# Norm factors applied by ScalarE to transposed rows, residuals through identity products, and five more whole weight units in each mix layer

## The chip, the cores and the metric

The kernel runs on one core of one Trainium2 chip. Time is device time in microseconds (us) from start to end of one execution; lower is better. The engines are TensorE (PE, with its weight loads PEld), VectorE (DVE), ScalarE (ACT), GpSimd (POOL) and SyncE (SP), which here issues most DMA transfers.

## What is computed

A batch of 256 tokens of width 1024 in fp32 goes through a hybrid state-space and attention block, and then through two layers. What this case touches is the second part, cut to its core:

```python
def layer_norm(x, g, b):
    xc = x - jnp.mean(x, axis=-1, keepdims=True)
    var = jnp.mean(xc * xc, axis=-1, keepdims=True)
    return xc * lax.rsqrt(var + LN_EPS) * g + b

h = layer_norm(x, ln_in_g, ln_in_b)
for i in range(2):
    proj = h @ w_in[i] + b_in[i]                       # a, g (512 each), q, k, v
    conv_out = conformer_conv(a, g, ...)               # gate, 31 taps, norm, silu
    attn_out = neighbourhood_attention(q, k, v, rpb[i])
    mix = jnp.concatenate([conv_out, attn_out], -1) @ w_out[i] + b_out[i]
    h = layer_norm(ALPHA * h + mix, ln1_g[i], ln1_b[i])
    f = swiglu(h, ...) if i == 0 else moe_swiglu(h, ...)   # 8 experts, top 2
    e = jax.nn.sigmoid(h @ ple_gate_w[i] + ple_gate_b[i]) * (p[i] @ ple_w[i])
    h = layer_norm(ALPHA * h + f + e, ln2_g[i], ln2_b[i])
```

## The kernel before

Tokens lie in two blocks of 128 rows (`tb`), and every norm works on one block at a time. Weights come from HBM in units of 1 MB (128 x 2048 numbers), in the order in which they are used. `prepare` (L286 to L301) has SP issue the load of a unit into one of three raw buffers; a buffer is free for a later unit when its last reader is done. Most units are *split*: ACT casts each half to a rounded part `whi` (L298), DVE subtracts to get the rest `wlo` (L299), and each product is three fast products (`mm3`, L317 to L319: `hi x whi`, `hi x wlo`, `lo x whi`). After a split the raw buffer is free again. Units listed in `WHOLE` stay as they are: the product is one plain fp32 product that reads the raw buffer (L329 in `f_out`, L351 in `t_jobs`). `f_out` makes 128 output columns for all 256 tokens with 8 such steps; `t_jobs` makes rows of 512 columns.

A mix layer takes 19 units, numbered here from 0 (in the second layer the same numbers plus 52): 0 the per-token embedding's matrix (`ple_prod`, result `pw`); 1 to 4 the gate's two halves `a` and `g`; 5 to 8 q, k, q, k; 9 and 10 v; 11 and 12 the attention half of `w_out`; 13 and 14 its convolution half; then 15 to 18, the embedding's gate (`ple`), 15 and 16 for its first 512 columns, 17 and 18 for the others. Whole before: 1 to 4, 15 and 16.

A norm (`layer_norm`, L854 on) runs on DVE: two BN_STATS, one aggregate, a reciprocal root from some ten operations on one column (`rstd`), and two operations for each 512 columns, `(x - mean) * gain` (L869) and `* r + offset` (L870). Then `to_f` has PE transpose the block (L876, tiles `tp`), ACT copies `tp` to `hh` (L878) and casts it to `hhi`, and DVE subtracts to get `hlo`; the next layer's products read those. This happens at four places: the first norm (`b1_merge`), the norm after each mix (`ln1`), and the norm after the dense layer (`ln2`).

In `mix` the taps of the convolution (`cv`, L1012, 120 per layer on DVE) run beside the attention on PE. The convolution's own norm (L865, tile `q`) then gives the convolution half of `cat`, and `w_out`'s products accumulate in four PSUM tiles (`acc`, `acc`, `acc`, `sm`); DVE adds them to the residual `r` (L1048). The MoE begins with the gate products (`hh`, units 15 and 16, then 17 and 18 split), the router, the choice of experts on DVE (`lg`, `sel`, `pos`, ..., `posp`, `gatep`), the gather of the chosen rows by one-hot products (L1416, `oh`), and the experts' products (L1568, `raw,xn`).

A scheduler puts the written code into an order for each engine, and each engine takes its instructions in that order; the code under `high_priority` goes ahead where it can. So what stands where on an engine is read from the order listing below, not from the code.

Of the kernel before, what the change touches and what calls it, by code (L numbers as in the profile page):

```python
# [157 lines left out]
def _host(i):  # L158
# [19 lines left out]
    for l in range(2):  # L178
        a["ws2"] += _stream_mix(g["w_in_2"][l], g["w_out_2"][l], g["ple_w_2"][l], g["ple_gate_w_2"][l])
        if l == 0:  # L180
            a["ws2"] += _stream_ffn(g["ffn_w1_2"][0], g["ffn_w3_2"][0], g["ffn_w2_2"][0])
        a["cols2"].append(np.concatenate(
            [_per_part(g["b_in_2"][l])] + [_per_part(g["conv_w_2"][l][t]) for t in range(31)]
            + [_per_part(g[n][l]) for n in ("conv_b_2", "conv_ln_g_2", "conv_ln_b_2")], 1))
# [37 lines left out]
WHOLE = [a + i for a in (0, 52) for i in (1, 2, 3, 4, 15, 16)]  # L222
# [19 lines left out]
class Kern:  # L242
    def __init__(self, tc, ctx, A, nring=(3, 3)):
# [13 lines left out]
        self.srcs += [(A["ws2"][i], i not in WHOLE) for i in range(A["ws2"].shape[0])]  # L257
# [141 lines left out]
    def first_block(self):  # L399
        tc, nc, A = self.tc, self.nc, self.A  # L400
        with ExitStack() as ctx:
# [35 lines left out]
            self.ple_load(0)  # L437
            with tc.tile_pool(name="mrg", bufs=1, side="right") as mp:
                return self.b1_merge(mp, yp, u, y, af, p1)
# [353 lines left out]
    def b1_merge(self, mp, yp, u, y, af, p1):  # L793
# [43 lines left out]
        with tc.high_priority():  # L837
            for tb in range(NT):
# [8 lines left out]
                self.layer_norm(x1, x1, g, b)  # L847
                self.to_f(x1, tb, hT)
# [23 lines left out]
    def to_f(self, h, tb, hT):  # L872
        for q in range(2):
# [28 lines left out]

    def ple_load(self, l):

        T = NT * P
        pT = self.hp.tile([P, 2, T], F32, name="pT")
        self.nc.scalar.dma_start(pT, self.A["pT"][l])
        self.p = self.hp.tile([P, 2, T], F32R, name="phi"), self.hp.tile([P, 2, T], F32R, name="plo")
        self.split(*self.p, pT)

    def ple_prod(self, l):

        phi, plo = self.p
        self.pw = self.hp.tile([P, NT, D], F32, name="pw")
        w = self.rows_unit(D)
        for tb in range(NT):
            for c in range(2):
                acc = self.bank([P, 512], "acc")
                for kk in range(2):
                    s = slice(tb * P, tb * P + P)  # L920
                    cc = slice(512 * c, 512 * c + 512)
                    self.mm3(acc, phi[:, kk, s], plo[:, kk, s], *w(kk, cc), kk == 0, kk == 1)
                self.nc.scalar.copy(self.pw[:, tb, 512 * c:512 * c + 512], acc)
        if l == 0:
# [10 lines left out]
    def mix(self, l, h, hT, h1):  # L935
# [3 lines left out]
        with ExitStack() as ctx:  # L939
            mp = ctx.enter_context(tc.tile_pool(name="mix", bufs=1, side="right"))  # L940
            cl = mp.tile([P, 156], F32, name="cols2")
            nc.scalar.dma_start(cl, A["cols2"][l])
# [57 lines left out]
            cat = (mp.tile([P, KD, T], F32R, name="cathi"), mp.tile([P, KD, T], F32R, name="catlo"))  # L1000
# [39 lines left out]
            for k0 in (4, 0):  # L1040
                self.t_jobs([(outs[c], self.rows_unit(512), [(k, k0 + k, k0 + k == 4, k0 + k == 3) for k in range(4)])
                             for c in range(2)], cat)
            nT = self.transposed()
            with tc.high_priority():
                for tb in range(NT):
                    for c in range(2):
                        cc = slice(512 * c, 512 * c + 512)
# [29 lines left out]
    def nb_out(self, mp, hd, L, v, cl, cat):  # L1077
# [14 lines left out]
        if e:  # L1092
            bv = cl[:, 16 + m:17 + m]
            nc.scalar.activation(cat[0][:, 4 + m], o, AF.Identity, bias=bv)
            nc.vector.scalar_tensor_tensor(cat[1][:, 4 + m], o, bv, cat[0][:, 4 + m].bitcast(F32),
# [18 lines left out]
    def dense(self, l, h, hT, h2):  # L1114
        tc, nc, A = self.tc, self.nc, self.A
        T = NT * P
        with ExitStack() as ctx:
# [32 lines left out]
            with tc.high_priority():  # L1150
                for tb in range(NT):
# [3 lines left out]
                    self.layer_norm(r[:, tb], h2[:, tb], g2, b2)  # L1155
                    self.to_f(h2[:, tb], tb, nT)
# [477 lines left out]
```

## Time and profile before

| | |
|---|---|
| median of 3 runs | 2001.63 us (2000.33 to 2001.87) |
| profiled execution | 1999.51 us, its span 1997.6 us |
| mean granted clock of TensorE | 0.983 of full speed |
| PE busy | 1903.2 us, 95% of the span |
| DVE busy | 1209.3 us, 61% |
| ACT busy | 874.3 us, 44% |
| chain that ended last | PE 84%, DMA 7%, DVE 6%, ACT 2% |

The first block fills the span up to some 490 us; then come mix 0 (to 623), the dense layer (to 846), mix 1 (to 969) and the MoE. "Busy" is the time in which an engine had an instruction at work; the granted clock is the share of full speed (2.4 GHz) that TensorE had. The chain that ended last is followed back from the last instruction, at each step to what it had waited for.

### The profile page before, as it was taken

Reading aid. Unit: us, or ns where it says so; the run is one execution under the profiler, and the core shown is the slowest. Engines: PE = TensorE matmul, PEld = TensorE weight load, DVE = VectorE, ACT = ScalarE, POOL = GpSimd, SP = SyncE. Lnnn points to the kernel's source line nnn. Section 1 sums busy time; section 2 is a strip of 40 time slices with the busy share of each in tenths; the row PEclk is TensorE's granted clock in tenths of the full one; section 3 lists DMA queues with packets and bytes.
Section 4 is the critical chain, followed back from the end, with each engine's and each line's share of the span. In section 5 each row is a group of like instructions: output and inputs, shape, how many; then the busy total and the mean of one; then the engine's idle time right before and its main releaser. Section 6 shows DMA issues by size and latency. Waiting matters only on the chain.

```text
span 1997.6 us, 27219 instructions
## 1 busy us (share of the span) xinstructions
PE 1903.2 (95%) x10378; PEld 1331.6 (67%) x10378; DVE 1209.3 (61%) x2185; ACT 874.3 (44%) x1411; POOL 8.9 (0%) x21
## 2 busy tenths in 40 slices
PE   7999999998989999998899899999999999999997
PEld 6988888897866999786553245444434444578875
DVE  6547799757896655589731125324433443788887
ACT  4655466344463544355311024323222323567764
POOL 0000000000000000000000000000000000000000
PEclk9999999999998999999899999999999999999998
DMA  5533444454524554563479998988998997998884
GB/s 215 187 138 117 148 153 164 164 200 175 214 97 146 197 194 172 184 215 109 197 279 410 421 421 327 377 346 349 365 383 334 376 373 297 380 347 322 334 329 161
DMA packets 82873, 515.18 MB, mean 258 GB/s; under 512 B 8688, under 2 KB 17568, under 8 KB 22960
## 3 DMA queue, kind: packets, MB, share of 16 engines
q1 hardware_dynamic: 69296, 494.57, 64.5%
q10 hardware_dynamic: 13440, 18.80, 2.9%
q8 instruction: 84, 1.38, 0.3%
q14 instruction: 53, 0.43, 0.1%
HBM read 512.24 MB, written 1.10 MB: 257 GB/s over the span
## 4 chain that ended last, share of the span: by engine, by line
PE 84%; DMA 7%; DVE 6%; ACT 2%; issue 1%; SPq 0%; DVEq 0%; ACTq 0%
PE acc L1568 15%; PE acc L317 14%; PE acc L318 14%; PE acc L319 14%; DMA raw<-in_wm 7%; PE sm L1568 3%; PE acc L329 3%; PE sm L317 2%; PE sm L318 2%; PE sm L319 2%; PE tp L1554 2%; PE acc L351 1%; DVE wlo L299 1%; PE acc L1416 1%; PE acc L1610 1%
## 5 line engine op out<-in xcount | busy, mean ns | idle before, releaser
L299 DVE TENSOR_TENSOR wlo<-raw,whi 128x1024 fp32r<-128x1024 f32 x490 | 583.6, 1221 | 166.5 <-ACT whi L298 165.1
L298 ACT CAST whi<-raw 128x1024 fp32r<-128x1024 f32 x490 | 495.3, 1048 | 188.2 <-PE acc L318 76.4
L1568 PE MATMUL acc<-raw,xn 128*64 128x512 f32 x1344 | 325.2, 599 | 10.0 <-DMA raw<-in_wm 9.8
L1558 DVE TENSOR_REDUCE g<-tp 128x256 f32<-128x512 f32 x84 | 57.9, 690 | 274.8 <-PE tp L1554 274.8
L1568 PEld LDWEIGHTS acc<-raw,xn 128*64 128x64 f32 x1344 | 94.1, 136 | 184.6 <-issue 154.8
L1527 ACT ACTIVATE eg<-acc 128x512 f32<-128x512 f32 x105 | 62.7, 597 | 331.5 <-PE acc L1568 282.2
L317 PE MATMUL acc<-uhi,whi 128*128 128x272 f32 (+1 forms) x576 | 168.8, 293 | 1.4 <-DVE rs_t L375 1.4
L318 PE MATMUL acc<-ulo,whi 128*128 128x272 f32 (+1 forms) x576 | 169.0, 293 | 0.0
L319 PE MATMUL acc<-uhi,wlo 128*128 128x272 f32 (+1 forms) x576 | 167.1, 290 | 0.0
L317 PE MATMUL acc<-hhi,whi 128*128 128x256 f32 x544 | 153.7, 282 | 0.0
L318 PE MATMUL acc<-hlo,whi 128*128 128x256 f32 x544 | 153.2, 282 | 0.0
L319 PE MATMUL acc<-hhi,wlo 128*128 128x256 f32 x544 | 152.6, 281 | 0.0
L317 PE MATMUL acc<-whi,xg 128*128 128x512 f32 x336 | 136.6, 407 | 5.7 <-ACT whi L298 5.7
L318 PE MATMUL acc<-wlo,xg 128*128 128x512 f32 x336 | 136.0, 405 | 1.1 <-DVE wlo L299 1.1
L319 PE MATMUL acc<-whi,xg 128*128 128x512 f32 x336 | 133.4, 397 | 0.0
L317 PEld LDWEIGHTS acc<-uhi,whi 128*128 128x128 f32 x576 | 110.1, 191 | 4.8 <-issue 2.5
L319 PEld LDWEIGHTS acc<-uhi,wlo 128*128 128x128 f32 x576 | 110.0, 191 | 1.8 <-issue 1.5
L318 PEld LDWEIGHTS acc<-ulo,whi 128*128 128x128 f32 x576 | 110.0, 191 | 1.8 <-issue 1.5
L1568 PE MATMUL sm<-raw,g 128*64 128x512 f32 x392 | 103.3, 605 | 1.7 <-DMA raw<-in_wm 1.7
L317 PEld LDWEIGHTS acc<-hhi,whi 128*128 128x128 f32 x544 | 103.2, 190 | 0.2
L318 PEld LDWEIGHTS acc<-hlo,whi 128*128 128x128 f32 x544 | 102.9, 189 | 0.2
L1012 DVE SCALAR_TENSOR_TENSOR cv<-u,cols,cv 128x256 f32<-128x256 f32 x240 | 101.7, 478 | 2.1 <-ACT cv L1010 1.3
(515 smaller groups left out, 3141.9 us busy)
## 6 DMA issues: line engine op xcount, KB each, us to landing
raw<-in_wm SPq DMA_DIRECT2D x336, 1024.0 KB, 7.7
raw<-in_ws SPq DMA_DIRECT2D x131, 1024.0 KB, 4.8
row<-in_rows ACTq DMA_DIRECT2D x9, 512.0 KB, 3.9
seg<-racs ACTq DMA_DIRECT2D x8, 512.0 KB, 3.9
rb<-in_rpb ACTq DMA_DIRECT2D x8, 512.0 KB, 3.4
ck<-rnck ACTq DMA_DIRECT2D x4, 544.0 KB, 3.7
x<-in_x SPq DMA_DIRECT2D x2, 512.0 KB, 5.0
gn<-in_rows ACTq DMA_DIRECT2D x4, 256.0 KB, 3.3
```

The lines of the kernel that those rows point to most:

```text
L298: nc.scalar.copy(hi, x)
L299: nc.vector.tensor_sub(lo, x, hi.bitcast(F32))
L317: nc.tensor.matmul(out, lhi, rhi, start=start, stop=False)
L318: nc.tensor.matmul(out, lhi, rlo, start=False, stop=False)
L319: nc.tensor.matmul(out, llo, rhi, start=False, stop=stop)
L329: self.nc.tensor.matmul(out, w.raw[:, k, c:c + P], x[2][:, k, t0:t1], start=k == 0, stop=k == n - 1)
L351: self.nc.tensor.matmul(outs[tb], x[2][:, kk, s], w.raw[:, k], start=start, stop=stop)
L1012: nc.vector.scalar_tensor_tensor(cv[:, m], u[:, m, t:t + T], w, cv[:, m], op0=OP.mult, op1=OP.add)
L1527: nc.scalar.activation(t, acc, AF.Copy if len(x) == 1 else AF.Silu)
L1554: i = self.nc.tensor.transpose(tp[:, k], a[:, k * P:k * P + P], self.ident)
L1558: self.nc.vector.tensor_reduce(g, tp.rearrange("p k (h s) -> p k s h", h=2), axis=AX.X, op=OP.add)
L1568: self.nc.tensor.matmul(out[h:h + 64], x[0][:, kx], w.raw[:, k], start=first and k < 2, stop=last and k >= n - 2)
```

## The change

1. The four norms use a new `layer_norm_f`. DVE makes the statistics as before, and `m = -mean * r`. ACT applies `x * r + m` (two operations of 128x512), PE transposes, and ACT applies gain and offset to the transposed tile, where they are numbers per partition (eight operations of 128x128 for each block, out of PSUM into `hh`). `hhi` and `hlo` are then made from `hh`. Rows that are needed untransposed get gain and offset later by `affine` on DVE. The numbers come as 48 more columns of `cols2`, loaded by `load_gains`.
2. In `mix`, four products with the identity put the residual into the PSUM tiles, in place of four DVE adds; BN_STATS reads PSUM.
3. `WHOLE` also has 0, 7, 8, 13 and 14, so the embedding rows `p` and the convolution half of `cat` need no split.
4. `LATE` keeps the first half's subtraction of unit 17 in program order.

```diff
-WHOLE = [a + i for a in (0, 52) for i in (1, 2, 3, 4, 15, 16)]
+WHOLE = [a + i for a in (0, 52) for i in (0, 1, 2, 3, 4, 7, 8, 13, 14, 15, 16)]
+LATE = [a + 17 for a in (0, 52)]
...
-    def prepare(self, src, split=True):
+    def prepare(self, src, split=True, late=False):
...
-            nc.vector.tensor_sub(lo, x, hi.bitcast(F32))
+            sub = nc.vector.tensor_sub(lo, x, hi.bitcast(F32))
+            if late and i == 0:
+                self.tc.keep_in_program_order(sub)
...
-                self.layer_norm(x1, x1, g, b)
-                self.to_f(x1, tb, hT)
+                self.layer_norm_f(x1, x1, tb, hT, 4)
+            for tb in range(NT):
+                self.affine(self.x1[:, tb], g, b)
...
+    def layer_norm_f(self, x, z, tb, hT, j):
...
+        xs = x if isinstance(x, list) else [x[:, :512], x[:, 512:]]
...
+            nc.vector.bn_stats(st[:, c], xs[c])
...
+        r = self.rstd(v)
...
+        nc.vector.scalar_tensor_tensor(m, mv[:, 0:1], -1.0, r, op0=OP.mult, op1=OP.mult)
+        s = slice(tb * P, tb * P + P)
+        for c in range(2):
+            nc.scalar.activation(z[:, 512 * c:512 * c + 512], xs[c], AF.Identity, scale=r, bias=m)
             tp = self.bank([P, 4, P], "tp")
             for k in range(4):
-                self.nc.tensor.transpose(tp[:, k], h[:, (4 * q + k) * P:(4 * q + k + 1) * P], self.ident)
-            hi, lo, whole = (t[:, 4 * q:4 * q + 4, tb * P:tb * P + P] for t in hT)
-            self.nc.scalar.copy(whole, tp)
-            self.split(hi, lo, tp)
+                at = (4 * c + k) * P
+                nc.tensor.transpose(tp[:, k], z[:, at:at + P], self.ident)
+            for k in range(4):
+                at = 4 * c + k
+                nc.scalar.activation(hT[2][:, at, s], tp[:, k], AF.Identity, scale=self.gbf[:, 8 * j + at:8 * j + at + 1],
+                                     bias=self.gbf[:, 8 * j + 8 + at:8 * j + 9 + at])
+        for c in range(2):
+            hi, lo, whole = (t[:, 4 * c:4 * c + 4, s] for t in hT)
+            self.split(hi, lo, whole)
+
+    def affine(self, x, g, b):
+        for c in range(2):
+            cc = slice(512 * c, 512 * c + 512)
+            self.nc.vector.tensor_mul(x[:, cc], x[:, cc], g[:, cc])
+            self.nc.vector.tensor_add(x[:, cc], x[:, cc], b[:, cc])
...
-                    self.mm3(acc, phi[:, kk, s], plo[:, kk, s], *w(kk, cc), kk == 0, kk == 1)
+                    self.nc.tensor.matmul(acc, self.p[:, kk, s], w.raw[:, kk, cc], start=kk == 0, stop=kk == 1)
...
-                nc.scalar.activation(cat[0][:, m], s, AF.Copy, scale=0.5)
-                nc.vector.scalar_tensor_tensor(cat[1][:, m], s, 0.5, cat[0][:, m].bitcast(F32),
-                                               op0=OP.mult, op1=OP.subtract)
+                nc.scalar.activation(cat[2][:, m], s, AF.Copy, scale=0.5)
...
-            for k0 in (4, 0):
-                self.t_jobs([(outs[c], self.rows_unit(512), [(k, k0 + k, k0 + k == 4, k0 + k == 3) for k in range(4)])
+            for tb in range(NT):
+                for c in range(2):
+                    nc.tensor.matmul(outs[c][tb], self.ident, r[:, tb, 512 * c:512 * c + 512], start=True, stop=False)
+            for i in range(2):
+                self.t_jobs([(outs[c], self.rows_unit(512), [(k, k, False, i == 1 and k == 3) for k in range(4)])
                              for c in range(2)], cat)
...
-                        nc.vector.tensor_add(r[:, tb, cc], r[:, tb, cc], outs[c][tb])
-                    self.layer_norm(r[:, tb], h1[:, tb], rows[1], rows[2])
-                    self.to_f(h1[:, tb], tb, nT)
+                    self.layer_norm_f([outs[c][tb] for c in range(2)], h1[:, tb], tb, nT, 0)
+                for tb in range(NT):
+                    self.affine(h1[:, tb], rows[1], rows[2])
```

Three places in the order of the engines' instructions, before and after. First PE at the end of mix 0, where `w_out`'s products end and the gate products (`raw,hh`) begin. Before:

```order
L318 MATMUL sm<-wlo,cathi 128x512
L319 MATMUL sm<-whi,catlo 128x512
L876 MATMUL tp<-cst,hb 128x128 x8
L351 MATMUL acc<-raw,hh 128x512 x3
L876 MATMUL tp<-cst,hb 128x128 x8
L351 MATMUL acc<-raw,hh 128x512 x13
```

After:

```order
L357 MATMUL acc<-raw,cat 128x512 x12
L357 MATMUL sm<-raw,cat 128x512
L900 MATMUL tp<-cst,hb 128x128 x8
L357 MATMUL sm<-raw,cat 128x512 x3
L357 MATMUL acc<-raw,hh 128x512 x6
L900 MATMUL tp<-cst,hb 128x128 x8
L357 MATMUL acc<-raw,hh 128x512 x10
```

The first block's eight transposes moved from behind all products of `w_out` to ahead of the last three, and three more gate products stand ahead of the second block's transposes.

Second DVE in the norm after mix 1 and in the MoE's choice of experts, where the four subtractions of units 17 and 18 (`wlo`) stand. Before, inside the second block's norm (`rs_` are the steps of the reciprocal root):

```order
L299 TENSOR_TENSOR wlo<-raw,whi 128x1024
L371 TENSOR_SCALAR rs_p<-rs_t 128x1
L299 TENSOR_TENSOR wlo<-raw,whi 128x1024
L372 TENSOR_TENSOR rs_p<-rs_p,rs_t 128x1
L299 TENSOR_TENSOR wlo<-raw,whi 128x1024
L373 SCALAR_TENSOR_TENSOR rs_y<-rs_p,rs_y 128x1
L299 TENSOR_TENSOR wlo<-raw,whi 128x1024
L366 SCALAR_TENSOR_TENSOR rs_t<-rs_y,lnv 128x1
```

After, behind the last steps of the choice of experts:

```order
L1308 COPY some<-gatep 128x8
L1313 TENSOR_TENSOR each<-ind,some 128x36
L1309 COPY some<-gatep 128x1
L1328 COPY gatep<-gatep 128x2
L1314 TENSOR_REDUCE posp<-each 128x4
L1313 TENSOR_TENSOR each<-ind,some 128x36
L303 TENSOR_TENSOR wlo<-raw,whi 128x1024
L1314 TENSOR_REDUCE gatep<-each 128x4
L303 TENSOR_TENSOR wlo<-raw,whi 128x1024 x3
```

All four moved behind the 80 or so operations of the router and the choice.

Third PE around the gather in the MoE. Before, the 48 split products of units 17 and 18 stand ahead of the gather (`oh,thi`); their last rows:

```order
L317 MATMUL acc<-whi,hhi 128x512
L318 MATMUL acc<-wlo,hhi 128x512
L319 MATMUL acc<-whi,hlo 128x512
L1416 MATMUL acc<-oh,thi 128x64 x4
L1416 MATMUL acc<-oh,tlo 128x64 x4
```

After, the gather ends and the split products follow, all but two of them:

```order
L1453 MATMUL acc<-oh,thi 128x64 x4
L1453 MATMUL acc<-oh,tlo 128x64 x4
L1453 MATMUL acc<-oh,thi 128x64 x4
L1453 MATMUL acc<-oh,tlo 128x64 x4
L324 MATMUL acc<-wlo,hhi 128x512
L325 MATMUL acc<-whi,hlo 128x512
L323 MATMUL acc<-whi,hhi 128x512
```

The gather went ahead, and 46 products that need `wlo` stand between it and the experts.

## Rows read from the trace of the kernel before

**Rows 1.** Busy us (x) of PE, PEld, DVE, ACT, POOL; PEclk, DMA, GB/s.
```profile
540.00:594.00 54.00, 49.03 (x275) 38.53 (x276) 50.81 (x156) 34.50 (x81) 0.00 (x0) 1.00 0.33 118
886.00:940.00 54.00, 48.20 (x262) 38.06 (x263) 50.38 (x153) 37.45 (x84) 0.00 (x0) 0.97 0.35 119
1012.00:1200.00 188.00, 173.77 (x858) 65.81 (x856) 37.47 (x77) 31.56 (x69) 0.00 (x0) 1.00 1.00 407
```

**Rows 2.** PE in order of time, rows behind waits: start, duration, [idle <-releaser].
```profile
496.67 1.94 PE L876 MATMUL tp<-cst,ha 128*128 128x128 f32 x8 [7.49 <-DVE ha L870]
598.76 0.41 PE L1028 MATMUL sm<-cst,q 128*128 128x128 f32 x2 [3.21 <-DVE rs_y L376]
621.48 1.97 PE L876 MATMUL tp<-cst,hb 128*128 128x128 f32 x8 [3.82 <-DVE hb L870]
623.27 4.47 PE L351 MATMUL acc<-raw,hh 128*128 128x512 f32 x6
844.48 1.29 PE L876 MATMUL tp<-cst,ha 128*128 128x128 f32 x8 [0.77 <-DVE ha L870]
948.69 0.66 PE L1028 MATMUL sm<-cst,q 128*128 128x128 f32 x2 [4.76 <-DVE rs_y L376]
980.58 1.94 PE L876 MATMUL tp<-cst,hb 128*128 128x128 f32 x8 [4.46 <-DVE hb L870]
```

**Rows 3.** PE in order of time, first and last rows of two runs.
```profile
535.78 0.28 PE L319 MATMUL acc<-hhi,wlo 128*128 128x256 f32 x1
538.25 0.28 PE L319 MATMUL acc<-hhi,wlo 128*128 128x256 f32 x1
606.30 0.39 PE L317 MATMUL acc<-whi,cathi 128*128 128x512 f32 x1
617.27 0.40 PE L319 MATMUL sm<-whi,catlo 128*128 128x512 f32 x1
```

**Rows 4.** The chain of work that ended last, whole products: start, duration.
```profile
628.61 11.16 PE acc L351 x26
845.78 27.89 PE acc L329 x128
```

**Rows 5.** Granted clock (PEclk) behind waits of PE, columns as in rows 1.
```profile
601.00:606.00 5.00, 5.00 (x13) 3.82 (x13) 2.80 (x7) 4.59 (x12) 0.00 (x0) 0.50 0.20 85
623.00:629.00 6.00, 6.00 (x19) 3.08 (x18) 5.83 (x14) 4.47 (x8) 0.00 (x0) 0.70 0.52 199
949.00:951.00 2.00, 1.82 (x8) 1.00 (x6) 0.46 (x1) 0.97 (x3) 0.00 (x0) 0.50 0.70 287
951.00:955.00 4.00, 4.00 (x13) 3.10 (x12) 2.28 (x6) 3.41 (x11) 0.00 (x0) 0.59 0.00 0
981.00:985.00 4.00, 3.81 (x12) 2.18 (x11) 3.93 (x7) 2.99 (x5) 0.00 (x0) 0.50 1.01 420
```

**Rows 6.** DVE in order of time, second norm before the MoE.
```profile
973.83 1.22 DVE L299 TENSOR_TENSOR wlo<-raw,whi 128x1024 fp32r<-128x1024 f32 x1
977.44 1.22 DVE L299 TENSOR_TENSOR wlo<-raw,whi 128x1024 fp32r<-128x1024 f32 x1
979.68 1.41 DVE L870 SCALAR_TENSOR_TENSOR hb<-hb,rs_y,row 128x512 f32<-128x512 f32 x2
```

**Rows 7.** ACT by line and shape, the rows nearest to the new activations.
```profile
L1031 ACT ACTIVATE cs<-sm,cols 128x256 f32<-128x256 f32 x8 | 4.1, 560 | 8.9 <-PE sm L1028 8.5 <-DVE catlo L1035 0.4
L1421 ACT COPY xn<-acc 128x128 f32<-128x128 f32 x24 | 5.7, 272 | 14.6 <-PE acc L1416 14.6
```

**Rows 8.** DMA issues of the whole run: KB each, median us to landing.
```profile
raw<-in_ws SPq DMA_DIRECT2D x131, 1024.0 KB, 4.8
```

**Rows 9.** DVE in order of time, the router's logits and the last routing result.
```profile
989.65 0.17 DVE L1192 COPY lg<-sm 128x16 f32<-128x16 f32 x1 [4.43 <-PE sm L1190]
1003.46 0.19 DVE L1277 TENSOR_REDUCE gatep<-each 128x4 f32<-128x36 f32 x1
```

**Rows 10.** PE in order of time, the MoE's first expert product.
```profile
1010.63 3.65 PE L1568 MATMUL acc<-raw,xn 128*64 128x512 f32 x16
```

More of the change, by code (lines that the diff above doesn't have):

```diff
@@ L183, in _host @@
             [_per_part(g["b_in_2"][l])] + [_per_part(g["conv_w_2"][l][t]) for t in range(31)]
-            + [_per_part(g[n][l]) for n in ("conv_b_2", "conv_ln_g_2", "conv_ln_b_2")], 1))
+            + [_per_part(g[n][l]) for n in ("conv_b_2", "conv_ln_g_2", "conv_ln_b_2")]
+            + [_per_part(g[n][l]) for n in ("ln1_g_2", "ln1_b_2", "ln2_g_2", "ln2_b_2")]
+            + [_per_part(g[n]) for n in ("ln_in_g_2", "ln_in_b_2")], 1))
         a["rows2"].append(np.stack([g[n][l] for n in ("b_out_2", "ln1_g_2", "ln1_b_2", "ple_gate_b_2",
@@ L256, in __init__ @@
         self.srcs = [(A["ws"][i],) for i in range(A["ws"].shape[0])]
-        self.srcs += [(A["ws2"][i], i not in WHOLE) for i in range(A["ws2"].shape[0])]
+        self.srcs += [(A["ws2"][i], i not in WHOLE, i in LATE) for i in range(A["ws2"].shape[0])]
         if "wm" in A:
@@ L437, in first_block @@
             self.ple_load(0)
+            self.load_gains(0)
             with tc.tile_pool(name="mrg", bufs=1, side="right") as mp:
@@ L870, in layer_norm @@
             nc.vector.scalar_tensor_tensor(out[:, c], out[:, c], r, b[:, c], op0=OP.mult, op1=OP.add)
-    def to_f(self, h, tb, hT):
-        for q in range(2):
+    def layer_norm_f(self, x, z, tb, hT, j):
+        nc = self.nc
+        xs = x if isinstance(x, list) else [x[:, :512], x[:, 512:]]
+        st = self.small.tile([P, 2, 6], F32, name="lnst")
+        for c in range(2):
+            nc.vector.bn_stats(st[:, c], xs[c])
+        mv = self.small.tile([P, 2], F32, name="lnmv")
+        nc.vector.bn_aggr(mv, st.rearrange("p a b -> p (a b)"))
+        v = self.small.tile([P, 1], F32, name="lnv")
+        nc.vector.tensor_scalar(v, mv[:, 1:2], LN_EPS, None, op0=OP.add)
+        r = self.rstd(v)
+        m = self.small.tile([P, 1], F32, name="lnm")
+        nc.vector.scalar_tensor_tensor(m, mv[:, 0:1], -1.0, r, op0=OP.mult, op1=OP.mult)
+        s = slice(tb * P, tb * P + P)
+        for c in range(2):
+            nc.scalar.activation(z[:, 512 * c:512 * c + 512], xs[c], AF.Identity, scale=r, bias=m)
             tp = self.bank([P, 4, P], "tp")
             for k in range(4):
-                self.nc.tensor.transpose(tp[:, k], h[:, (4 * q + k) * P:(4 * q + k + 1) * P], self.ident)
-            hi, lo, whole = (t[:, 4 * q:4 * q + 4, tb * P:tb * P + P] for t in hT)
-            self.nc.scalar.copy(whole, tp)
-            self.split(hi, lo, tp)
+                at = (4 * c + k) * P
[12 more added lines that the diff above has]
+            self.nc.vector.tensor_add(x[:, cc], x[:, cc], b[:, cc])
     def rowk(self, src, off, name="row"):
@@ L901, in second_block, with load_gains @@
             nc.sync.dma_start(out[tb], other[:, tb])
+    def load_gains(self, l):
+        self.gbf = self.hp.tile([P, 48], F32, name="gbf")
+        self.nc.scalar.dma_start(self.gbf, self.A["cols2"][l, :, 156:])
     def ple_load(self, l):
[L905 to L909, printed above, removed]
+        self.p = self.hp.tile([P, 2, NT * P], F32, name="pT")
+        self.nc.scalar.dma_start(self.p, self.A["pT"][l])
     def ple_prod(self, l):
-        phi, plo = self.p
         self.pw = self.hp.tile([P, NT, D], F32, name="pw")
@@ L998, in mix @@
                 nc.scalar.copy(v[:, tb], vp[tb])
-            cat = (mp.tile([P, KD, T], F32R, name="cathi"), mp.tile([P, KD, T], F32R, name="catlo"))
+            cat = tuple(mp.tile([P, 4, T], F32 if n == "cat" else F32R, name=n) for n in ("cathi", "catlo", "cat"))
             for hd in range(8):
@@ L1093, in nb_out @@
             bv = cl[:, 16 + m:17 + m]
-            nc.scalar.activation(cat[0][:, 4 + m], o, AF.Identity, bias=bv)
-            nc.vector.scalar_tensor_tensor(cat[1][:, 4 + m], o, bv, cat[0][:, 4 + m].bitcast(F32),
+            nc.scalar.activation(cat[0][:, m], o, AF.Identity, bias=bv)
+            nc.vector.scalar_tensor_tensor(cat[1][:, m], o, bv, cat[0][:, m].bitcast(F32),
                                            op0=OP.add, op1=OP.subtract)
@@ L1154, in dense @@
                         nc.vector.tensor_add(r[:, tb, cc], r[:, tb, cc], outs[c][tb])
-                    self.layer_norm(r[:, tb], h2[:, tb], g2, b2)
-                    self.to_f(h2[:, tb], tb, nT)
+                    self.layer_norm_f(r[:, tb], h2[:, tb], tb, nT, 2)
+                for tb in range(NT):
+                    self.affine(h2[:, tb], g2, b2)
             return nT
```

7 lines of the change are left out of this document (4 added, 3 removed).

## Prediction

> **What bounds the kernel now.** The table says PE is busy for 95% of the span, so I first asked the windows by stage where the other 5% lies. In the MoE the DMA is the limit: 188 us at a DMA share of 1.00 [rows 1]. In the mix layers DVE is nearly full, 50.81 and 50.38 of 54 us, and PE idles 4.97 and 5.80 us there [rows 1]. Then I read PE in order of time for rows with an idle time in brackets: the reader sees waits of 7.49 us at the first norm, 3.21 and 3.82 us at the end of mix 0, 0.77 us behind the dense layer, 4.76 and 4.46 us in mix 1, each released by DVE in a norm [rows 2]. Last I read the granted clock behind those waits: after PE has stood still the next stretches run at 0.50 to 0.70, where 0.50 is the lower level, 1.2 GHz of 2.4 [rows 5]. So every norm costs its wait and some half-speed work behind it. The change works on these waits, and pays for it with more PE work.
>
> **Prices.** Split products of 512 columns start 0.2334 us apart: 10.97 us over 47 steps, so three take 0.70 us. Split products of 256 columns start 0.1176 us apart (2.47 over 21), so the 24 of one f_out take 2.82 us [rows 3]. Whole products leave two records each: the 16 gate products of mix 0 are the x6 and x26 records from 623.27 on [rows 2, 4]. A whole product of 512 columns is then 11.16/13 = 0.858 us, and a whole f_out (8 products) 27.89/8 = 3.49 us [rows 4].
>
> **PE work added.** Per layer: units 7 and 8, four f_outs, 4 x (3.49 - 2.82) = +2.7 us; units 13 and 14, 16 products, 16 x (0.858 - 0.70) = +2.5; four identity products, 4 x 0.858 = +3.4; unit 0, 8 products, +1.3. That is +9.9 us per layer, 19.8 in all. Removed from DVE per layer: ten weight subtractions of 1.22 us [rows 6] and the four residual adds; from ACT ten casts. The 32 operations that applied gains ahead of the transposes of the four norms become 32 multiplies and adds behind them. What the lighter DVE is worth has to be read place by place, from the waits.
>
> **First norm: -1.2 us** (bounds -2.5 to +0.5). Before, PE waits 7.49 us [rows 2]. Two subtractions leave the chain of the first token block (-2.4); the longer pw products hide in the wait, which is far longer than 1.3 us. But the first block's four affine operations, 0.70 us each by half of the pair of 1.41 [rows 6], are queued on DVE in the second block's chain of small dependent steps; where they fill its waits they cost nothing, otherwise 2.8. I take 1.2 of it.
>
> ACT now applies the norm. No row has a 128x128 activation with both operands per partition. The bounds are the 128x128 copy, 0.27 us, and the 128x256 activation with both operands, 0.56 [rows 7]; I take 0.40, so 3.2 us for a block's eight. The consumer needs one tile per whole product, and a product of 512 columns takes 0.858 us: eight activations run ahead of it, and I charge nothing beyond the first. At 0.56 the last tile would come 1.3 us later at each place, still behind products. The Trainium skill, ScalarE: Activation LUTs, "What ACT_TABLE_LOAD costs", gives 186 ns plus 0.833 ns per column, 93 ns per pointer operand, with 93 ns overlapped: an estimate of 0.39 us a piece here; the same page, "Rules for kernel authors", would leave multiplies and adds on VectorE, which speaks against the change. By the page the eight take 3.1 us, and the sum stays the same; the 0.56 row fits its formula (0.585).
>
> **Mix 0 up to the gate products: -2.8 us** (bounds -5 to 0). Added +8.6. Against it: the wait of 3.21 us for the convolution's norm goes [rows 2]; the four subtractions of units 13 and 14 no longer stand in its chain and the four of 7 and 8 no longer ahead of it, 9.8 us less for DVE. Before, half-speed work followed that wait: 5 us at 0.50, a loss of 2.5 us [rows 5]. From the last w_out product (617.27 + 0.40) to the first gate product (623.27) stood 5.6 us [rows 2, 3]; now the first block's transposes stand after its own products and ahead of the last three of the second block, so I expect 1.1 us of transposes and waits of 0.5 and 0.7, 2.3 in all: -3.3. And three identity products (2.6 us) stand in front of softmax's transposes, where PE idled in part of those 4.97 us [rows 1]; 2.4 us of the added work falls into waits. 8.6 - 3.2 - 2.5 - 3.3 - 2.4 = -2.8.
>
> **Gate products of mix 0: +1.6** (bounds 0 to +4). Units 13 to 15 now hold all three raw buffers until PE has used them. Unit 18 takes that of unit 15, free only at the 12th of 16 gate products. Landing takes 4.8 us [rows 8], then come a cast and a subtraction (1.22), and on DVE the four ple operations stand ahead of it. I get 2.3 us of waiting where before unit 18 was ready early; the 6 us at 0.70 behind the norm [rows 5] lost 1.8 us, of which 0.7 is saved.
>
> **Dense end: +0.7** (-0.5 to +2). The pw products grow by 1.3 us and only 0.77 us of wait is there to hide them [rows 2]; the two subtractions that left are worth the rest.
>
> **Mix 1 up to the gate products: -1.0** (-4 to +1). The same +8.6; against it the wait of 4.76 [rows 2], the slow work behind it, 2 x 0.50 + 4 x 0.41 = 2.6 [rows 5], and 2.2 into the 5.80 us idle [rows 1]. The norm's own wait was short here, so nothing is gained at it.
>
> **From there to the MoE's first product: +2.5** (-2 to +5). Before, four subtractions of units 17 and 18 stood inside the second block's norm (the first at 973.83, the last at 977.44, the gains at 979.68 [rows 6]), and PE waited 4.46 us [rows 2]; but then 48 products ran beside the routing. Now that norm is some 5 us sooner, so the wait shrinks to 1.5 (-3.0), and 4 us at 0.50 [rows 5] are saved (-2.0). But the order puts the four subtractions behind the whole routing. It took 1003.46 + 0.19 - 989.65 = 14.0 us from the logits to the last result [rows 9]. With logits at 986.3 that ends at 1000; a subtraction; then the 46 products that are left, 46 x 0.2334 = 10.7, and 1.3 us for a low clock after some 6 us of PE standing still: 1013.2 against 1010.63 [rows 10].
>
> **The sum.** -1.2 - 2.8 + 1.6 + 0.7 - 1.0 + 2.5 = -0.2 us. The rest of the MoE keeps its order; its buffers are full when it starts in either kernel, so I pass the shift on as it is. On the profiled execution's 1999.51 that is 1999.3; the median of the runs, 2001.63, lies 2.1 above it, so I forecast 2001.4. What a measurement here can tell from no change is about 0.2%, 4 us.
>
> **Rivals.** (1) Faster. The late weights are hidden: the gather's PE work and the earlier norm cover them. Then +1.6 and +2.5 become -0.7 and -4, the first norm reaches its -2.5: about -10 us, 1992. For it: 9.8 us less DVE work in a stage that DVE fills. Against it: the order of DVE as shown.
>
> (2) Slower, by one mechanism: in each mix layer unit 17's first cast stands on ACT ahead of the second block's gains, and ACT takes its work in order. The raw buffer of unit 17 comes free with the last w_out product, so the cast waits for a landing. At 4.8 us [rows 8] it is done about 6 us after that product, when the second block's transposes end; it decides from a landing of 6 us on. At 7.5 us the gains come 2 to 3 us late in each layer, PE stands and falls to the low clock (1.5 more each): +8, 2009.5.
>
> (3) The shift does not pass through the MoE: with the DMA at 1.00 [rows 1], a prefetch that starts later costs its own time. Two units fewer are issued ahead of the expert numbers; at 407 GB/s, 2.6 us each: +5, 2006.5.
>
> **How the numbers follow.** My forecast 0.40, rival 1 0.32, rival 2 0.17, rival 3 0.11. The bounds of the six terms, added as squares, give about 6 us to either side; with the rivals, whose times lie at both ends, 1991 to 2010. The likeliest case's own range is 1997 to 2006. Faster 0.33, within 0.2% 0.40, slower 0.27: rival 1 gives nearly all of the first, rivals 2 and 3 the third.
>
> **What would show it.** Right: the waits for the convolution's norm gone, no 0.50 behind them; the gate products of mix 0 starting near 619; PE standing for unit 18 near 637 and some 6 us ahead of unit 17's products in mix 1, with the first expert product at 1010 to 1011. Wrong: a wait for ACT gains longer than 1.5 us, unit 17's cast waiting for DMA, or an expert product later than 1014 or sooner than 1006.

## The result and the profile after

The changed kernel is slower: 2017.1 us median (2011.17 to 2023.58, 9 runs) against 2001.87 (1996.27 to 2007.99, 9 runs of the kernel before on the same chips), a ratio of 1.0067 with a 95% interval of 1.0048 to 1.0086. The forecast was 2001.4 in 1991 to 2010, so the time lies outside the range. The profiled execution's span is 2016.5 us; before it was 1997.6.

To see where the time went I read the starts of a few products in both traces and took differences, beginning with the last product of the first block, whose code did not change (482.15 before, 483.44 after):

| stretch | before | after | difference | forecast |
|---|---|---|---|---|
| last product of the first block to the first f_out of mix 0 | 16.3 | 15.6 | -0.7 | -1.2 |
| to the first gate product of mix 0 | 124.8 | 119.7 | -5.1 | -2.8 |
| to the first f_out of mix 1 | 222.5 | 222.2 | -0.3 | +2.3 |
| to the first gate product of mix 1 | 123.2 | 125.2 | +2.0 | -1.0 |
| to the first expert product | 41.6 | 49.7 | +8.1 | +2.5 |
| to the second gather | 33.9 | 42.5 | +8.6 | 0 |
| to the end of the span | 953.1 | 958.3 | +5.2 | 0 |

The last line differs by several us between profiled executions of kernels with the same code there (953 to 961 in the kernels below), so its 5.2 cannot be read as an effect. The fourth stretch's +2.0 cannot be read as one either: the same stretch is 121.1 us in first_ring below and 125.0 in late_first_only, two kernels with the same code there. The +8.1 and the +8.6 are the loss.

The windows after, with the columns of [rows 1]:

```profile
540.00:594.00 54.00, 50.47 (x234) 37.48 (x233) 46.03 (x152) 32.34 (x78) 0.00 (x0) 1.00 0.38 137
594.00:630.00 36.00, 35.98 (x118) 19.64 (x117) 19.37 (x57) 17.02 (x38) 0.00 (x0) 1.00 0.19 66
886.00:940.00 54.00, 50.65 (x224) 37.31 (x223) 42.31 (x134) 32.26 (x78) 0.00 (x0) 0.96 0.37 137
949.00:955.00 6.00, 6.00 (x21) 3.58 (x20) 0.35 (x2) 0.76 (x2) 0.00 (x0) 1.00 0.00 0
985.00:1012.00 27.00, 22.58 (x97) 18.11 (x96) 17.80 (x92) 3.26 (x10) 0.00 (x0) 0.68 0.33 124
1012.00:1200.00 188.00, 166.17 (x801) 63.68 (x801) 36.09 (x75) 30.00 (x66) 0.00 (x0) 0.96 0.91 370
```

The norms of the mix layers went as meant: DVE fell from 50.81 to 46.03 and from 50.38 to 42.31 of 54 us, and 949 to 955 runs at full clock where [rows 5] show 0.50 and 0.59. The loss stands in 985 to 1012: PE is busy for 22.58 of 27 us at a granted clock of 0.68.

PE in order of time after, the rows that answer to [rows 2, 10] and those with new waits:

```profile
497.24 1.97 PE L900 MATMUL tp<-cst,ha 128*128 128x128 f32 x8 [4.67 <-ACT ha L896]
...
596.12 0.41 PE L1065 MATMUL sm<-cst,q 128*128 128x128 f32 x2
...
618.73 5.31 PE L357 MATMUL acc<-raw,hh 128*128 128x512 f32 x12
...
637.63 0.73 PE L323 MATMUL acc<-whi,hhi 128*128 128x512 f32 x2 [1.08 <-ACT whi L302]
...
884.12 2.54 PE L1100 MATMUL acc<-k,q 128*128 128x256 f32 x4 [3.21 <-ACT k L1025]
...
966.12 7.03 PE L357 MATMUL acc<-raw,hh 128*128 128x512 f32 x16
...
974.48 1.32 PE L900 MATMUL tp<-cst,hb 128*128 128x128 f32 x8 [1.33 <-ACT hb L896]
...
1002.48 1.07 PE L1453 MATMUL acc<-oh,tlo 128*128 128x64 f32 x4 [0.35 <-ACT xn L1458]
...
1015.78 3.65 PE L1605 MATMUL acc<-raw,xn 128*64 128x512 f32 x16
...
1027.04 3.68 PE L1605 MATMUL acc<-raw,xn 128*64 128x512 f32 x8 [7.60 <-DMA raw<-in_wm]
```

The reader is to see three things. The wait of 7.49 us at the first norm is 4.67, and the convolution's transposes (596.12) and the gate products of mix 0 (618.73) start without one. Unit 18's cast is waited for at 637.63, but for 1.08 us. And at the MoE the gather ends at 1002.48 + 1.07, the first expert product comes at 1015.78, and then PE stands for 7.60 us, released by a DMA. Before, this wait was 0.80 us.

What holds the products of units 17 and 18 ahead of the first expert product is on two engines. DVE in order of time:

```profile
985.78 0.17 DVE L1229 COPY lg<-sm 128x16 f32<-128x16 f32 x1 [0.63 <-PE sm L1227]
...
1001.98 1.22 DVE L303 TENSOR_TENSOR wlo<-raw,whi 128x1024 fp32r<-128x1024 f32 x1
...
1003.21 3.48 DVE L303 TENSOR_TENSOR wlo<-raw,whi 128x1024 fp32r<-128x1024 f32 x3
```

The logits are there at 985.78, and the subtractions of units 17 and 18 (`wlo`) follow only from 1001.98 on, behind the routing, as the order listing showed; the first of them ends at 1003.20. On PE the gather, which stands ahead of the products that read `wlo`, ends at 1003.55. The two end within 0.4 us of each other, so neither holds the products alone. What holds the second wait is in the chain that ended last, from the last product of unit 18 to the next expert product:

```profile
1015.62 0.25 PE acc L325
1015.89 0.70 DVE ha L1144
1016.62 0.64 ACT ha L1145
1017.28 0.70 DVE ha L1146
1018.01 0.44 DVE ha L1147
1018.47 0.70 DVE hb L1148
1019.22 7.68 DMA raw<-in_wm
1027.04 3.68 PE acc L1605 x8
```

After the last gate product (1015.62) come the four operations of `ple` on DVE and ACT, and only when the last of them ends (`hb`, 1018.47 + 0.70) does the load of the third expert unit begin. That unit's buffer is `raw4`, which the code makes when it closes the pools that the embedding's gate (`ple`) works in: it lies in that memory. The chain is 3.6 us of `ple` and 7.68 us of transfer, and the only work that PE has beside it is the first two units, 3.65 us. Before, the gather stood on PE beside `ple`'s last operations. The gather and the load in the chain that ended last there, and between them DVE's last operation of `ple`:

```profile
1006.42 3.15 PE acc L1416 x28
...
1009.11 0.69 DVE L1112 SCALAR_TENSOR_TENSOR hb<-hb,ha 128x512 f32<-128x512 f32 x1
...
1009.88 5.16 DMA raw<-in_wm
```

and PE's row for the third unit:

```profile
1015.08 1.94 PE L1568 MATMUL acc<-raw,xn 128*64 128x512 f32 x8 [0.80 <-DMA raw<-in_wm]
```

There the gather (1006.42 to 1009.57) covered the operations of `ple`, the last of which ended at 1009.80, and the first two units, from 1010.63 on, covered the transfer but for 0.80 us. The transfer itself took 5.16 us, 2.5 less than after; of the 6.8 us between the two waits that leaves some 4.3 for the lost cover. With the eight products behind the wait, 3.68 us against 1.94 before, that makes the +8.6. Why the same load takes longer after is open.

### The profile page after: what moved, and what is told of

Read it like the earlier page. It is cut to its first block, busy times and chain, and to the rows that moved or that the text cites. A ratio compares the mean times of both kernels' runs of the same rounds, so it can differ in the third digit from the quotient of the medians.

```text
span 2016.5 us, 27012 instructions
## 1 busy us (share of the span) xinstructions
PE 1928.0 (96%) x10282; PEld 1329.8 (66%) x10282; DVE 1180.9 (59%) x2155; ACT 878.0 (44%) x1453; POOL 8.9 (0%) x21
## 4 chain that ended last, share of the span: by engine, by line
PE 80%; DMA 9%; DVE 7%; ACT 3%; issue 1%; SPq 0%; DVEq 0%; ACTq 0%
PE acc L1605 15%; PE acc L323 13%; PE acc L324 13%; PE acc L325 13%; DMA raw<-in_wm 7%; PE sm L1605 4%; PE sm L324 2%; PE sm L323 2%; PE sm L325 2%; DVE cv L1049 2%; PE acc L335 2%; PE acc L357 2%; PE tp L1591 2%; DVE wlo L303 1%; DMA raw<-in_ws 1%; PE acc L1453 1%
## 5 line engine op out<-in xcount | busy, mean ns | idle before, releaser
L303 DVE TENSOR_TENSOR wlo<-raw,whi 128x1024 fp32r<-128x1024 f32 x470 | 558.7, 1220 | 166.9 <-ACT whi L302 165.1
L302 ACT CAST whi<-raw 128x1024 fp32r<-128x1024 f32 x470 | 474.4, 1049 | 176.7 <-PE acc L324 74.5
L324 PE MATMUL acc<-hlo,whi 128*128 128x256 f32 x480 | 134.3, 280 | 0.0
L323 PE MATMUL acc<-hhi,whi 128*128 128x256 f32 x480 | 134.3, 280 | 0.0
L325 PE MATMUL acc<-hhi,wlo 128*128 128x256 f32 x480 | 134.0, 279 | 0.0
L323 PEld LDWEIGHTS acc<-hhi,whi 128*128 128x128 f32 x480 | 90.2, 188 | 0.1
L324 PEld LDWEIGHTS acc<-hlo,whi 128*128 128x128 f32 x480 | 90.1, 188 | 0.1
```

What stands on the lines that cost most here:

```text
L303: sub = nc.vector.tensor_sub(lo, x, hi.bitcast(F32))
L323: nc.tensor.matmul(out, lhi, rhi, start=start, stop=False)
L324: nc.tensor.matmul(out, lhi, rlo, start=False, stop=False)
L325: nc.tensor.matmul(out, llo, rhi, start=False, stop=stop)
```

## The experiments

Two theories were set against each other. A: the late subtractions at the start of the MoE are the loss. B: the whole units' and identity products' 19.8 us of PE work are. Every kernel was timed in five rounds beside the kernel before; ratios are to that kernel, with a 95% interval. The kernels came in three groups, each with its own runs of the kernel before, so kernels of different groups are compared by their ratios.

**late_first_only**: the changed kernel without the second layer's entry in `LATE`.

```diff
-LATE = [a + 17 for a in (0, 52)]
+LATE = [17]
```

> The changed kernel, with LATE naming unit 17 of the first layer only. In the order of the engines nothing but the start of the MoE differs: the four subtractions of units 17 and 18 stand ahead of the router's logits again, their 48 products ahead of the gather. Theory A (the late subtractions at the start of the MoE are the loss): 15 to 19 us less than the changed kernel, 2 to 5 us less than the kernel before, the first expert product near 1008 and no wait of over 2 us behind it. Theory B (the added PE work of the whole units and the identity products is the loss): within 4 us of the changed kernel, 2013 or more.

Measured: 1996.38 us, ratio 0.9965 (0.9951 to 0.9979), 20.7 us below the changed kernel and 6 below the kernel before. On DVE the last operation of `ple`:

```profile
1004.11 0.68 DVE L1148 SCALAR_TENSOR_TENSOR hb<-hb,ha 128x512 f32<-128x512 f32 x1
```

and PE's rows for the first and the third unit:

```profile
1005.82 3.65 PE L1605 MATMUL acc<-raw,xn 128*64 128x512 f32 x16
1011.77 1.94 PE L1605 MATMUL acc<-raw,xn 128*64 128x512 f32 x8 [2.29 <-DMA raw<-in_wm]
```

The chain of `ple` ends at 1004.79 and not at 1019.17, and PE waits 2.29 us. The two stretches that lost 8.1 and 8.6 us measure 36.8 and 35.4: 12.9 and 7.1 less than after, 20.0 in all, close to the difference of the medians. Theory A holds, and theory B falls as the cause of the loss. The gain is a little more than I had set (15 to 19, and 2 to 5 under the kernel before), and so is the wait (2 us).

**before_late**: the kernel before, with that one entry added to it.

```diff
+LATE = [69]
...
-            nc.vector.tensor_sub(lo, x, hi.bitcast(F32))
+            sub = nc.vector.tensor_sub(lo, x, hi.bitcast(F32))
+            if late and i == 0:
+                self.tc.keep_in_program_order(sub)
```

> The kernel before, with the first subtraction of unit 17 of the second layer kept in program order and nothing else. Theory A: 10 to 18 us slower than before, with a wait of PE for a weight load of 5 us or more behind the first expert unit. Theory B: within 4 us of the kernel before.

Measured: 2009.27 us, ratio 1.0036 (1.0021 to 1.0051), 7 us slower. PE's rows for the first and the third expert unit:

```profile
1009.99 3.65 PE L1572 MATMUL acc<-raw,xn 128*64 128x512 f32 x16
...
1019.44 3.68 PE L1572 MATMUL acc<-raw,xn 128*64 128x512 f32 x8 [5.79 <-DMA raw<-in_wm]
```

The entry alone makes the kernel before slower, with a wait of 5.79 us of the same kind. It costs less there than in the changed kernel, and less than the 10 us that I had as the lower end: its first expert product is only 1.3 us later (42.9 us after the gate's start, against 41.6). Behind that product the entry costs much the same in both kernels: 41.2 us to the second gather against 33.9 here, 7.3 more, and 7.1 more there. The difference lies ahead of it, and the traces show where. In the kernel before the four subtractions stood in the second block's norm, where PE waited 4.46 us [rows 2]; with the entry they leave it, and the wait is gone:

```profile
974.13 1.29 PE L880 MATMUL tp<-cst,hb 128*128 128x128 f32 x8
```

The logits come 15.1 us after the first gate product (982.12), where before they came 20.7 us after it, and that pays for most of the late start. The changed kernel had no such wait to lose: it is 0.23 us in late_first_only.

**no_late**: the changed kernel with no entry at all (`LATE = []`).

> The changed kernel with an empty LATE. Theory A: within 4 us of the kernel with the first layer's entry alone, so 15 us or more below the changed kernel; what the first layer's entry does is 0 to 3 us either way. Theory B: within 4 us of the changed kernel.

Measured: 1997.22 us, ratio 0.9976 (0.9961 to 0.999). The first layer's entry is worth nothing that these runs tell apart from nothing.

**ring_last**: the changed kernel, with the buffer `raw4` last in the ring.

```diff
-            self.raws = [raw4] + self.raws
+            self.raws = self.raws + [raw4]
```

> The changed kernel, with the raw buffer that takes the memory of the embedding's gate (raw4) last in the ring of buffers and not first, so that the third expert unit needs another buffer. Theory A in its full form (the third unit waits for the last gate operation on DVE, then for a transfer): the wait of 7.60 us goes, 6 to 12 us less than the changed kernel, the first expert product still near 1015. If the wait comes from transfers that are slow or from the order of the queue alone: within 3 us of the changed kernel. Theory B: within 3 us too.

Measured: 2007.82 us, ratio 1.0031 (1.0019 to 1.0043), 9.3 us below the changed kernel. PE's row at the first expert product:

```profile
1014.28 5.37 PE L1605 MATMUL acc<-raw,xn 128*64 128x512 f32 x24
```

All 24 records of the first three units stand in one row from 1014.28 on, with no wait among them: the third unit no longer uses the memory of `ple`. The first expert product is as late as after. So the 7.60 us and what followed come with the buffer's chain, and the rest, some 11 us, is the late start.

**first_ring**: both edits, `LATE = [17]` and `raw4` last.

> The kernel with LATE for the first layer alone, and raw4 last in the ring of buffers. There PE still waited 2.29 us for the third expert unit. If that wait was the chain of the gate's last operation and a transfer: 1 to 4 us less than with LATE for the first layer alone (1996.38), so 1992 to 1995. If the MoE's transfers swallow it: within 1 us of 1996.4.

Measured: 1993.95 us, ratio 0.9963 (0.9951 to 0.9975). The median lies where the first branch had it, 2.4 us below late_first_only, but by the ratios the two are the same (0.9965): without the late start the buffer's place in the ring makes no difference that these runs can tell.

**old_norms**: late_first_only with the norm's old path.

```diff
-        for c in range(2):
-            nc.scalar.activation(z[:, 512 * c:512 * c + 512], xs[c], AF.Identity, scale=r, bias=m)
...
+        for c in range(2):
+            cc = slice(512 * c, 512 * c + 512)
+            nc.vector.scalar_tensor_tensor(z[:, cc], xs[c], mv[:, 0:1], g[:, cc], op0=OP.subtract, op1=OP.mult)
+            nc.vector.scalar_tensor_tensor(z[:, cc], z[:, cc], r, b[:, cc], op0=OP.mult, op1=OP.add)
```

> The kernel with LATE for the first layer alone, with the norms' gains and offsets applied by DVE ahead of the transposes as before, and one copy, cast and subtraction for four tiles; residuals by identity and whole units as in the change. If the norms' new path pays: 4 to 9 us more than 1996.4, with waits of PE at the first norm and behind mix 0 and mix 1. If it does not: within 2.5 us of 1996.4.

Measured: 1992.78 us, ratio 0.996 (0.9945 to 0.9975). The new path brings nothing that can be told from nothing. PE's wait at the first norm in this kernel:

```profile
494.09 1.94 PE L897 MATMUL tp<-cst,ha 128*128 128x128 f32 x8 [4.55 <-DVE ha L893]
```

It is 4.55 us with the old path and 4.67 with the new one: what shortened the 7.49 was the weight work that left DVE, not the activations.

**conv_split** and **qk_split**: late_first_only with two units of each layer split again.

```diff
-WHOLE = [a + i for a in (0, 52) for i in (0, 1, 2, 3, 4, 7, 8, 13, 14, 15, 16)]
+WHOLE = [a + i for a in (0, 52) for i in (0, 1, 2, 3, 4, 7, 8, 15, 16)]
```

is conv_split, where the convolution half of `cat` is split as before too, and

```diff
-WHOLE = [a + i for a in (0, 52) for i in (0, 1, 2, 3, 4, 7, 8, 13, 14, 15, 16)]
+WHOLE = [a + i for a in (0, 52) for i in (0, 1, 2, 3, 4, 13, 14, 15, 16)]
```

is qk_split.

> The kernel with LATE for the first layer alone, with units 13 and 14 split in both layers (five units whole per layer less two; the convolution half of cat split too). If DVE's work in the convolution's norm is what counts: 2 to 8 us more than 1996.4, with the wait ahead of the convolution's transposes back. If PE's work is what counts: 5 us less, the price of 32 whole products over split ones.

> The kernel with LATE for the first layer alone, with units 7 and 8 split in both layers. If DVE's work in the attention stretch is what counts: 1 to 6 us more than 1996.4. If PE's work is what counts: 5 us less, the price of eight whole f_outs over split ones.

Measured: conv_split 1992.22 us, ratio 0.995 (0.9934 to 0.9967); qk_split 1991.61 us, ratio 0.9944 (0.9929 to 0.9959). Each pair, split again, is 3 to 4 us faster by the ratios, though the intervals touch that of late_first_only. That fits PE's work as what counts, as long as the other pair is whole: neither trace has a wait of 0.5 us or more ahead of the convolution's transposes, in either layer. The overlap of the intervals leaves it short of shown.

**both_split**: both pairs split again.

> The kernel with LATE for the first layer alone, with units 7, 8, 13 and 14 split again in both layers; unit 0 whole, norms and identity products as in the change. Alone, each pair gave some 3 to 4 us by the ratios. If the two add up (PE's work counts in each place): 5 to 8 us less than with all five whole, a ratio of 0.992 to 0.994. If DVE then becomes the limit of the stretch again: a ratio of 0.9955 or more, and the wait ahead of the convolution's transposes back.

Measured: 1996.54 us, ratio 0.9963 (0.995 to 0.9975). The two do not add up. PE ahead of the convolution's transposes in mix 0:

```profile
599.98 0.66 PE L1065 MATMUL sm<-cst,q 128*128 128x128 f32 x2 [5.49 <-DVE rs_y L382]
```

and its windows around it:

```profile
540.00:594.00 54.00, 52.69 (x285) 39.48 (x285) 50.31 (x155) 35.38 (x81) 0.00 (x0) 1.00 0.32 115
601.00:606.00 5.00, 4.99 (x13) 3.00 (x13) 2.06 (x6) 4.01 (x10) 0.00 (x0) 0.50 0.15 59
```

A wait of 5.49 us is back (5.04 in mix 1), with 50.31 of 54 us of DVE work in the stretch ahead of it and half the clock behind it. One pair whole takes the wait away; of the second the traces show only more products.

**both_split_ring**: the same with `raw4` last.

> The same, with raw4 last in the ring of buffers. If the wait for the third expert unit is still there without it: 1 to 3 us less than the same kernel with raw4 first. If the order of the loads has healed it already: within 1.5 us of it.

Measured: 1998.08 us, ratio 0.9967 (0.9955 to 0.998): the same as both_split.

**residual_dve**: late_first_only with the residual added by DVE.

```diff
-                    nc.tensor.matmul(outs[c][tb], self.ident, r[:, tb, 512 * c:512 * c + 512], start=True, stop=False)
...
-                    self.layer_norm_f([outs[c][tb] for c in range(2)], h1[:, tb], tb, nT, 0)
+                    for c in range(2):
+                        cc = slice(512 * c, 512 * c + 512)
+                        nc.vector.tensor_add(r[:, tb, cc], r[:, tb, cc], outs[c][tb])
+                    self.layer_norm_f(r[:, tb], h1[:, tb], tb, nT, 0)
```

> The kernel with LATE for the first layer alone, with the residual added by DVE in SBUF ahead of the norm as before, in place of the four identity products of each layer. If the identity products pay (they fill waits, and DVE's adds stand on the path of the norm): 1 to 5 us more than that kernel, a ratio of 0.997 to 0.999 to the kernel before. If PE's added 3.4 us per layer are the greater: 2 to 6 us less, a ratio of 0.9935 to 0.9955.

Measured: 1990.33 us, ratio 0.9943 (0.993 to 0.9957). The identity products cost some 4 us by the ratios, though here too the intervals overlap a little; as two layers' products are 6.9 us of PE, some 2.5 of these fell into waits or were paid back by the adds that left DVE. It is one of the fastest kernels measured, some 12 us below the kernel before.

**before_ring**: the kernel before with `raw4` last.

> The kernel before with raw4 last in the ring of buffers and nothing else. It waited only 0.80 us for the third expert unit, so the theory that this wait is the ring's price gives 0 to 2 us less than before. If the ring helps for another reason (the DMA's order in the MoE): 3 us or more.

Measured: 2003.65 us, ratio 1.0002 (0.9988 to 1.0016). A wait of 0.80 us was not worth anything, as expected.

## Why the prediction was wrong, step by step

**The step that failed** is "From there to the MoE's first product: +2.5 us", with the sentence behind the sum that "The rest of the MoE keeps its order; its buffers are full when it starts in either kernel, so I pass the shift on as it is". In place of +2.5 and 0 the trace shows +8.1 and +8.6, and the experiments give 20 us to the one entry of `LATE`.

The first term can be taken apart, counted from the first gate product of mix 1. The prediction had the logits 17.3 us behind it (986.3, against 968.99 in the kernel before; the two gains that it names, 3.0 and 2.0, would even give 15.7), the late products 14.9 us behind the logits and the first expert product 12.0 behind those. Measured are 19.7, 17.8 and 12.2. So the price of the 46 products held, and the two steps ahead of them were 2.4 and 2.9 us short.

The first of these is PE's order. The second block's norm kept PE waiting for 1.33 us, near the 1.5 forecast, but ten records of gate products now stand ahead of the router's products, where two stood before. The rows behind the second block's transposes, before and after:

```profile
982.71 2.08 PE L351 MATMUL acc<-raw,hh 128*128 128x512 f32 x2 [0.19 <-ACT hh L878]
...
976.44 4.56 PE L357 MATMUL acc<-raw,hh 128*128 128x512 f32 x10 [0.64 <-ACT hh L903]
```

Eight records are four products, 3.4 us at the prediction's price: the norm's gain went into them, and the logits came only 1.0 us sooner after the first gate product than before (19.7 against 20.7).

The order listing had shown the four late subtractions, and I priced them; three more things were missed.

First, the gather. I had it run beside the routing and the products follow at 1001.2. In the trace its last records are at 1002.48 to 1003.55, and the products follow at 1003.54 in the chain that ended last. Its groups go one at a time: each waits until ACT has copied, or DVE has added, the result of the one before. Two products of unit 17, a DVE add and the group behind it:

```profile
986.24 1.03 PE L323 MATMUL acc<-whi,hhi 128*128 128x512 f32 x2
...
994.85 0.29 DVE L1460 TENSOR_TENSOR xn<-xn,acc 128x128 f32<-128x128 f32 x1 [0.77 <-PE acc L1453]
...
995.19 1.06 PE L1453 MATMUL acc<-oh,thi 128*128 128x64 f32 x4 [0.45 <-DVE xn L1460]
```

The code has three PSUM tiles named `acc` (`bank`). The two products of unit 17 that need no `wlo` were begun at 986.24, one for each block, and hold two of them until the late products are done, so the gather has one. In the kernel before it stood behind all those products, and three of its groups started within 0.9 us (1006.26, 1006.62, 1007.14). This is read from the traces and the code and was not tried by itself. The adds stand in DVE's order among the routing's operations, so DVE waits for PE there too, 0.77 us above and 0.94 and 1.83 elsewhere, and the routing takes 16.2 us up to the first subtraction where I had 14.0 for the whole. And the gather runs at half the clock, window by window, columns as in rows 1:

```profile
992.00:996.00 4.00, 3.55 (x24) 3.33 (x24) 1.37 (x9) 0.64 (x2) 0.00 (x0) 0.50 0.00 0
996.00:1000.00 4.00, 2.84 (x13) 2.44 (x12) 2.89 (x26) 0.53 (x2) 0.00 (x0) 0.50 0.00 2
1000.00:1004.00 4.00, 3.19 (x13) 2.83 (x14) 3.91 (x22) 0.27 (x1) 0.00 (x0) 0.50 0.00 0
```

The clock had fallen over 988 to 992 (0.71), behind a wait of 1.22 us for DVE at 988.48, and it stayed at 0.50 over the first of the late products (1004 to 1006.5). The Trainium skill, TensorE: Matmul & The Clock Gate, "Part 1: The HAM clock gate", says that the clock gate is throttled by default and that activity releases it. The trace agrees in part: late_first_only, whose gather has no such waits, has 1.00 over 985 to 1012, but in the three windows above PE was at work for 9.58 of 12 us and the clock stayed low.

Second, what waits behind the late products. I asked who waits for the subtractions (PE's 46 products) and not who waits for those products' result. The third expert unit's buffer lies in `ple`'s memory, so a late `ple` means a late load: 3.6 us of `ple`, which the gather covered before, and 7.68 us of transfer. ring_last shows it: 9.3 us come back when that unit gets another buffer.

Third, I took the buffers to be "full when it starts". They were not: the third unit of the row was missing, in both kernels. The shift was passed on, but new time was added to it.

**The rivals.** Rival 3 had the right place, a load in front of the experts that costs its own time, but another mechanism (two units fewer issued ahead) and 5 us; nothing shows that the two units mattered. Rival 2, unit 17's first cast on ACT waiting for its landing ahead of the second block's factors, did not come in mix 0: the gate products there run from 618.73 on with no such wait. In mix 1 it came, at a small price:

```profile
972.70 1.04 ACT L302 CAST whi<-raw 128x1024 fp32r<-128x1024 f32 x1 [4.58 <-DMA raw<-in_ws]
973.65 0.77 ACT L896 ACTIVATE hb<-acc,lnm,rs_y 128x512 f32<-128x512 f32 x1
```

ACT stands 4.58 us for the load, and PE's wait of 1.33 us for `hb` (974.48) comes behind it; where late_first_only has 0.23. So the 1.5 us forecast for that wait was near the measured one by luck: it was meant for DVE's norm. Unit 17's cast waiting for a DMA was one of the signs of being wrong. The same kind of wait came once more in ACT's queue, earlier in mix 1:

```profile
881.61 1.99 ACT L302 CAST whi<-raw 128x1024 fp32r<-128x1024 f32 x2 [3.88 <-DMA raw<-in_ws]
883.51 0.47 ACT L1025 ACTIVATE k<-acc,cols 128x256 f32<-128x256 f32 x1
```

The cast of a split unit waits 3.88 us for its load and stands ahead of the last output of k, and PE waits 3.21 us for that (884.12): units 7 and 8, now whole, hold their raw buffers longer, which fits. In qk_split, where they are split, the cast ahead of the last k has no such wait, but first_ring, where they are whole, has a wait of only 0.72 us there; profiled executions with whole units 7 and 8 show from none to 3.2 us. So the cause stays open. Rival 1, faster, is what the rest of the change is: without the entry of the second layer the kernel is 6 us faster than before.

**What was right.** The mix layers' waits went as listed, and the gate products of mix 0 come 5.1 us sooner where I had 2.8. The convolution's wait does depend on DVE's load: it is back in both_split. The wait for unit 18 was 1.08 us, not 2.3. The first norm is -0.7 for -1.2, by the subtractions that left DVE, as the sum had it: PE's wait there is 4.55 us with the norm's old path and 4.67 with the new one (old_norms). The price of a gain, which no row had shown, can now be read from ACT in order of time:

```profile
615.87 2.91 ACT L903 ACTIVATE hh<-tp,gbf 128x128 f32<-128x128 f32 x8 [0.27 <-PE tp L900]
```

Eight take 2.91 us, 0.364 for each, where I took 0.40; one lasts 0.472 us by the mean of all 64, so they start 0.348 apart. The Trainium skill, ScalarE: Activation LUTs, "What ACT_TABLE_LOAD costs", gives 0.39 by its formula: a little high, the measurement decides. The advice in "Rules for kernel authors", on the same page of the Trainium skill, to leave multiplies and adds to VectorE made no difference that could be measured here (old_norms).

**Where the gain went.** Without the entry of the second layer, the kernels with one pair split or with the residual on DVE measured 10 to 12 us below the kernel before. Of the parts that were tried apart, one pair of whole units paid, by the wait that comes back without it, and it hardly mattered which; the second pair and the identity products cost some 3 to 4 us each by the ratios, at the edge of the intervals; the norms' new path did nothing that these runs can tell. Unit 0 was not tried by itself. The entry of the second layer took 20 us, more than all the rest gave.

## What to carry to other kernels

When an order listing shows that an operation moved behind a long chain, follow what comes behind it to the end: the products that need it, the operations that read those, and the buffers that these hold, up to the next load that takes their memory. What was begun ahead of the chain counts too: a product that waits half done keeps its PSUM tile, and other work has one fewer. A buffer in the memory of a pool that is closed late is such a wait, though no name in the order listing shows it.

Moving work from one engine to another pays until the second one is what is waited for: either of two like edits took a wait of 5.49 us away, and with both in place one seems only to add its own price. Try such edits one at a time.

An instruction that pins an operation in place can be harmless in one layer and costly in the next, where other work follows it.

## What was not expected of the hardware

A gather whose groups waited 0.35 or 0.45 us each ran at a granted clock of 0.50, the lower level of 1.2 GHz, for 12 us (992 to 1004 above) with PE at work for 9.58 of them. The same gather without such waits ran at full clock before (1006 to 1010; 1.00 over 985 to 1012). I had looked for the low clock only behind long waits.
